# Down projection in seven products: second group's operands requested step by step, last operands of the first group ahead of a residual quarter

## The chip, the cores and the metric

The kernel runs on one core of a Trainium2 chip. The metric is the device time of one execution in microseconds. The times of the kernel before are those of three runs; the profile is that of one execution.

## What is computed

One step of a two-layer streaming encoder for 1024 prompt tokens and 32 sample tokens (1056 in all) of 1024 features, in float32. Layer 0 mixes with a matrix memory, layer 1 with banded attention; each is followed by the same kind of MLP, and the part of the reference that matters here is the MLP of layer 1 with its residual and norm:

```
x = layer_norm(ALPHA * x + (1 + g1) * y, p['ln_g'][l, 0], p['ln_b'][l, 0])
u = x * (1 + sc2) + sh2
f = jnp.square(jax.nn.relu(u @ p['w_up'][l])) @ p['w_down'][l]
x = layer_norm(ALPHA * x + (1 + g2) * f, p['ln_g'][l, 1], p['ln_b'][l, 1])
```

`w_up` is 1024 x 4096, `w_down` 4096 x 1024.

## The kernel before

Every float32 product is made of three matmuls on rounded halves: the high half of the weight with the high and the low half of the moving operand, then the low half of the weight with the high half. The halves are made by `split` (lines 87 to 90): a copy on ScalarE (L89) and a subtraction on VectorE (L90).

The MLP of layer 1 is `mlp7`. It cuts the 4096 hidden features into 16 blocks of 256 and the 1056 tokens into four quarters of 264, two quarters to a token pair. A 2 x 2 block product is made in seven products (`PRODS`, L1095) instead of eight. The up products write, for each hidden block, seven forms of the squared ReLU to DRAM (`hd`, L1172 and L1177), as high and low halves. The down products of blocks 0 to 13 follow in five groups (`GRP`, L1092): group 0 has two blocks, groups 1 to 4 have three each. Blocks 14 and 15 are done in the plain way at the end.

A **unit** (`unit`, L1394) is one group and one quarter `m` of the output features; there are four units to a group, numbered 0 to 3 for group 0, 4 to 7 for group 1 and so on. A unit has seven steps, and in each step a product for each of the two token pairs: six matmuls a product in group 0, nine in the others. In the very first unit the pair tp1 is not started until all seven products of tp0, the first pair in order, are done; everywhere else the pairs alternate. Behind each product VectorE adds the bank, times a gate, into the residual (`add_gated_at`, L986; the tile `ACX`), and a later step accumulates into the same bank, so it waits for that add.

Three kinds of transfers feed a unit, all of them from SP's queue, in the queue's order:

- the **operands** `fx`: fourteen sets for a group, one for each pair and form, loaded from `hd` by `Rooms.load` (L1107 to 1119). A set of group 0 is 128 x 1056 numbers, one of the others 128 x 1584. They are put into rooms: 56 slots in all, of which group 0 uses 28 and each other group 42. Nine sets of group 1 fit beside group 0; the other five take the rooms that unit 3 gives back, product by product (`after`, L1465). `fill` (L1383) asks for as many sets as there are rooms, or for as many as its last argument allows. A set whose slots lie in two tiles takes two transfers.
- the **weights** `rdn_d`: two transfers to a unit (L1248), into a ring of three buffers. `forms` (L1243 to 1275) makes the seven weight forms of them: differences on VectorE (L1264 to 1267), then splits. The tile names carry the unit's number: `rdn_d_3_0` is the first half for unit 3, `wf_d_3_4` the split forms 4 and 5 for it. A buffer comes free when VectorE has read it; the first half's last reader is L1266, the second half's the split of form 6.
- the **residual**, in four quarters (`reload`, L1932): the first two during the up products, the third (`L.reload(2)`) at the end of the up products, in `up_end` (L1420), the fourth (`L.reload(3)`) at the start of the down products (L1456). Units 0 and 1 add into the first half, unit 2 into the third quarter, unit 3 into the fourth.

TensorE's order is the order of the code (`manual_schedule`). The order of SP, VectorE and ScalarE is chosen by a scheduler when the kernel is built, from the order of the code and a model of the durations; on the chip each engine then works strictly in that order.

Of the kernel before, what the change touches and what calls it, by code (L numbers as in the profile page):

```python
# [75 lines left out]
def trunk_kernel(ctx: ExitStack, tc: tile.TileContext, a, o):  # L76
# [668 lines left out]
    for h in range(1, NH):  # L745
        unit = [0]
# [377 lines left out]
    def mlp7(L):  # L1124
# [204 lines left out]
        preps, got = {}, {}  # L1329

        def prep(n):
            if n < len(makers):
                preps[n] = makers[n]()
                next(preps[n])

        def advance(n, i):

            if n + 1 in preps and i in (0, 1, 3, 5):
                got[n + 1] = next(preps[n + 1])
            if i == 2:  # L1340
                prep(n + 2)
# [37 lines left out]
        fx, nfx, f4s = {}, {}, []  # L1379
# [3 lines left out]
        def fill(g, into, most=99):  # L1383

            kg = GRP[g][1]
            while want and len(rooms.free) >= kg and most:
                most -= 1
                if g >= len(GRP) - 3:
                    late = g == len(GRP) - 1 or g == len(GRP) - 2 and len(into) < 10
                    rooms.free.sort(key=lambda r: any(r[0] is t for t in f4s[:3]) == late)  # L1390
                tp, f = want.pop(0)
                into[tp, f] = rooms.load(hd[g][tp][f], kg)

        def unit(g, m, phases, ws, step, after):  # L1394


            kg = GRP[g][1]
            for tps in phases:
                ps = {}
                for i, (w, f, b, c, q) in enumerate(PRODS):  # L1400
                    for tp in tps:
                        first = (tp, b) not in ps
                        if first:
                            ps[tp, b] = mm(f"dn{l}_{g}_{m}_{tp}_{b}")
                        p = ps[tp, b][:, :QN]
                        for k in range(kg):
                            t, s0 = fx[tp, f][k]
                            for n_, (wl, xl) in enumerate(((0, 0), (0, 1), (1, 0))):
                                nc.tensor.matmul(p, ws[w][:, wl, k], t[:, s0, xl], start=first and k + n_ == 0,  # L1409
                                                 stop=k == kg - 1 and n_ == 2, skip_group_check=not first)  # L1410
                        L.add((2 * tp + q) * QN, QN, p, L.gate, 2 * m + c)
                        after(tp, f)
                        flow.tick(QN * kg / 768)
                    if tps is phases[-1]:
                        step(i)
# [2 lines left out]
        prep(1)  # L1418
        got[0] = next(preps[0])
        def up_end():  # L1420
            L.reload(2)
            for t in L.rooms(tp1):
                rooms.add(t)
            fill(0, fx)
        lone = max(j for j, (_, tp) in enumerate(jobs) if tp == tp0)
        sevens = {}
        with tc.manual_schedule(engines={mybir.EngineType.PE}):
# [16 lines left out]
        nu = len(seq)  # L1444
# [7 lines left out]
        with tc.manual_schedule(engines={mybir.EngineType.PE}):  # L1452
            for i, (g, m, phases) in enumerate(units):
                more = g + 1 < len(GRP)
                if i == 0:
                    L.reload(3)  # L1456
                if i == 0:
                    rooms.add(ring.tile([P, KG, 2, QN], F32R, tag="wc", name=f"fx_w{l}", bufs=6))
                    fill(0, fx)
                if m == 1 and more:  # L1460
                    want += [(tp, f) for f in order_f for tp in L.pairs]
                if m == (2 if g else 1) and more:
                    fill(g + 1, nfx)

                def after(tp, f):  # L1465
                    if m == 3 and more:
                        rooms.free += fx[tp, f]
                        fill(g + 1, nfx)
                unit(g, m, phases, got[nu + i], lambda j: advance(nu + i, j), after)
                if m == 3:  # L1470
                    assert not want
                    fx, nfx = nfx, {}
# [70 lines left out]
    for gi, grp in enumerate(((0, 1, 2), (3,))):  # L1543
        ws = {pr: [wblock(f"q{pr}_{half}", wq, 512 * half, 256 * pr) for half in range(2)] for pr in grp}
        for ti, (t0, n) in enumerate(TBS):
# [7 lines left out]
            for fc in [f for pr in grp for f in (2 * pr, 2 * pr + 1)]:  # L1553
                g, r = fc // 2, 2 * (fc % 2)
# [73 lines left out]
    for t in range(NT):  # L1628
        if t % 2 == 0 and t < 8:
            flow.add(cached_keys(t // 2))  # L1630
        m = P if t < NT - 1 else TS
# [279 lines left out]
    class L1:  # L1911
# [49 lines left out]
        def after(blk):  # L1961
            t0, n = blk
            tiles = [(t, min(P, t0 + n - t)) for t in range(t0, t0 + n, P)]
            flow.add(norm_out(tiles, L1.put_out, L1.next_y, L1.gb, blk == L1.blocks[-1]), TAIL[0])
    mlp7(L1)
    flow.finish()
    psD_cm.__exit__(None, None, None)
# [36 lines left out]
```

## Time and profile before

| what | us |
|---|---|
| median of 3 runs (lowest, highest) | 2462.29 (2459.95, 2464.19) |
| the profiled execution, its time | 2464.7 |
| its span, first to last instruction | 2462.6 |
| TensorE busy (share of the span) | 2387.9 (97%) |
| VectorE busy | 1918.8 (78%) |
| ScalarE busy | 1089.9 (44%) |
| first product of group 0 to the end of the down groups | 2077.5 to 2393 |
| mean granted TensorE clock | 0.989 |

The time of an execution is a little longer than its span, which counts from the first to the last instruction. In the rows of the profile an operation is named by its line, engine and tiles (written tile, arrow, read tiles); in the view in order of time a bracket at the end of a row gives the idle time of the engine just before it and what ended that time. A matmul's row carries the length of a run of matmuls, and `x` their number; matmuls overlap at their ends, so that the pace is read from one start to the next. `SPq` is SP issuing transfers: the row shows when one is issued, not when it lands.

### The profile page before, as it was taken

What the parts mean: (1) busy time and instruction counts of PE and PEld (TensorE: products, weight loads), DVE (VectorE), ACT (ScalarE), POOL (GpSimd) and SP (SyncE); (2) the same over time, 40 slices, a digit from 0 to 9 for tenths busy, and PEclk for the clock granted to TensorE, in tenths of its full rate; (3) what the DMA queues carried; (4) which work ended last, traced back from release to release, by engine and by line L of the source; (5) the groups of instructions that cost most, each with busy time, mean ns of one, the idle gap of its engine ahead of it and who ended that gap; (6) DMA issues with size and microseconds to landing.
All of it is one profiled execution on the core that took longest, in us unless ns stands there. A gap on an engine that the chain in (4) does not pass through costs nothing.

```text
span 2462.6 us, 42910 instructions
## 1 busy us (share of the span) xinstructions
PE 2387.9 (97%) x16580; PEld 2296.7 (93%) x16580; DVE 1918.8 (78%) x4340; ACT 1089.9 (44%) x2264; POOL 167.3 (7%) x315
## 2 busy tenths in 40 slices
PE   7999999999999999999999999999999999799997
PEld 4999999999999999999999977889999998799997
DVE  4899999788679679677497666755998888677778
ACT  4644456382212212212257566763776776122212
POOL 0211100000000000000001134410000000000003
PEclk9999999999999999999999999999999999899999
DMA  8433223313224224234123220051586789856642
GB/s 296 125 110 102 77 92 111 131 35 105 83 88 128 88 92 129 86 95 149 45 78 99 74 63 1 18 134 41 175 282 216 253 300 332 305 216 229 228 160 72
DMA packets 251504, 335.17 MB, mean 136 GB/s; under 512 B 12824, under 2 KB 201644, under 8 KB 250276
## 3 DMA queue, kind: packets, MB, share of 16 engines
q1 hardware_dynamic: 251300, 332.42, 41.2%
q8 instruction: 131, 2.15, 0.4%
q14 instruction: 73, 0.60, 0.1%
HBM read 255.50 MB, written 79.24 MB: 136 GB/s over the span
## 4 chain that ended last, share of the span: by engine, by line
PE 76%; DVE 11%; DMA 4%; ACT 2%; issue 2%; POOL 1%; SPq 0%; DVEq 0%; ACTq 0%; POOLq 0%
PE dn L1409 11%; PE up L1300 9%; PE up L118 5%; PE dn L119 5%; PE dn L118 5%; PE up L120 5%; PE up L119 5%; PE dn L120 5%; PE pv L1744 3%; PE s L1687 2%; PE pt L1722 2%; PE o L118 1%; PE o L119 1%; PE o L120 1%; PE op_b L118 1%
## 5 line engine op out<-in xcount | busy, mean ns | idle before, releaser
L1409 PE MATMUL dn<-fx,wf_d 128*128 128x264 f32 x2016 | 257.7, 288 | 17.2 <-DVE ACX L986 12.8
L1409 PEld LDWEIGHTS dn<-fx,wf_d 128*128 128x128 f32 x2016 | 252.8, 191 | 19.0 <-ACT wf_d L89 13.3
L119 PE MATMUL dn<-h,w_dn 128*128 128x384 f32 (+1 forms) x768 | 249.5, 325 | 0.0
L118 PE MATMUL up<-U,w_up 128*128 128x384 f32 (+1 forms) x768 | 249.2, 324 | 0.0
L119 PE MATMUL up<-U,w_up 128*128 128x384 f32 (+1 forms) x768 | 247.9, 323 | 0.0
L118 PE MATMUL dn<-h,w_dn 128*128 128x384 f32 (+1 forms) x768 | 247.8, 323 | 0.0
L120 PE MATMUL up<-U,w_up 128*128 128x384 f32 (+1 forms) x768 | 247.6, 322 | 0.0
L120 PE MATMUL dn<-h,w_dn 128*128 128x384 f32 (+1 forms) x768 | 247.3, 322 | 0.0
L986 DVE SCALAR_TENSOR_TENSOR ACX<-dn,ada,ACX 128x264 f32<-128x264 f32 (+5 forms) x400 | 160.7, 427 | 56.2 <-PE dn L1409 43.4
L238 DVE SCALAR_TENSOR_TENSOR aacc<-rada,cs,aacc 128x256 f32<-128x256 f32 x448 | 190.3, 478 | 0.0
L986 DVE SCALAR_TENSOR_TENSOR acc<-dn,ada,acc 128x384 f32<-128x384 f32 (+2 forms) x256 | 119.4, 486 | 47.6 <-PE dn L120 46.1
L1025 ACT ACTIVATE r<-up 128x384 f32<-128x384 f32 (+1 forms) x96 | 44.2, 462 | 243.5 <-PE up L120 238.2
L119 PEld LDWEIGHTS dn<-h,w_dn 128*128 128x128 f32 x768 | 144.5, 188 | 0.2 <-DVE h L1028 0.2
L120 PEld LDWEIGHTS dn<-h,w_dn 128*128 128x128 f32 x768 | 144.5, 188 | 0.0
L120 PEld LDWEIGHTS up<-U,w_up 128*128 128x128 f32 x768 | 144.3, 188 | 0.0
L118 PEld LDWEIGHTS up<-U,w_up 128*128 128x128 f32 x768 | 144.2, 188 | 0.1
L119 PEld LDWEIGHTS up<-U,w_up 128*128 128x128 f32 x768 | 144.2, 188 | 0.0
L118 PEld LDWEIGHTS dn<-h,w_dn 128*128 128x128 f32 x768 | 144.0, 187 | 0.2
L1300 PE MATMUL up<-u,wf_u 128*128 128x264 f32 x1056 | 139.5, 284 | 1.3 <-ACT wf_u L89 0.6
L1300 PEld LDWEIGHTS up<-u,wf_u 128*128 128x128 f32 x1056 | 132.6, 188 | 1.9 <-ACT wf_u L89 0.8
L1027 DVE TENSOR_TENSOR r<-r 128x384 f32<-128x384 f32 (+1 forms) x96 | 50.0, 523 | 102.3 <-ACT h L1026 101.9
L89 ACT CAST w_up<-raw_up 128x1024 fp32r<-128x1024 f32 x52 | 54.3, 1046 | 138.4 <-DMA raw_up<-in_w_up_dram 113.9
(386 smaller groups left out, 6569.4 us busy)
## 6 DMA issues: line engine op xcount, KB each, us to landing
rada<-in_w_ada_dram SPq DMA_DIRECT2D x64, 512.0 KB
hd<-HL SPq DMA_DIRECT2D x28, 1056.0 KB
raw_up<-in_w_up_dram SPq DMA_DIRECT2D x52, 512.0 KB
fx<-hd SPq DMA_DIRECT2D x50, 528.0 KB
hd<-HM SPq DMA_DIRECT2D x28, 792.0 KB
raw_dn<-in_w_down_dram SPq DMA_DIRECT2D x36, 512.0 KB
ada_room<-in_w_ada_dram SPq DMA_DIRECT2D x32, 512.0 KB
rdn_u<-in_w_up_dram SPq DMA_DIRECT2D x32, 512.0 KB
```

The costliest lines, as they stand in the source:

```text
L89: nc.scalar.copy(dst_h, src)
L118: nc.tensor.matmul(ps, wh, mov(0, k), start=(k == 0), stop=False)
L119: nc.tensor.matmul(ps, wh, mov(1, k), start=False, stop=False)
L120: nc.tensor.matmul(ps, wl, mov(0, k), start=False, stop=(k == nk - 1))
L238: nc.vector.scalar_tensor_tensor(acc[:, cnd], raw[:, k], sc, acc[:, cnd], op0=ALU.mult, op1=ALU.add)
L986: nc.vector.scalar_tensor_tensor(xs, ps[:, off + o:off + o + mm_], gate[:, fc, cnd:cnd + 1], xs, op0=ALU.mult, op1=ALU.add)
L1027: nc.vector.tensor_mul(r, r, r)
L1300: nc.tensor.matmul(p, self.ws[w][:, wl, k], moving(f, tp, xl, k), start=first and k + n_ == 0, stop=k == 3 and n_ == 2, skip_group_check=n ...
L1409: nc.tensor.matmul(p, ws[w][:, wl, k], t[:, s0, xl], start=first and k + n_ == 0, stop=k == kg - 1 and n_ == 2, skip_group_check=not first)
L1687: nc.tensor.matmul(s[:, b, :w], qst, kk[i][:, g, k0 + j0:k0 + j0 + w], start=(i == 0), stop=(i == 1))
L1722: nc.tensor.transpose(pt[:kp, j - j0, pr * P:(pr + 1) * P], ps_[pr][:, j * P:j * P + kp], ident)
L1744: nc.tensor.matmul(pv[64 * e:64 * e + 64, :nq], V[:kp, vt0 + j, g * 64:(g + 1) * 64], pts[e][:kp, j, :nq], start=(j == 0), stop=(j == nt - 1))
```

## The change

In `up_end` the third quarter of the residual is asked for after the rooms of the second token tile have been filled, no longer before. In the loop over the units, the `fill` for the second group (`g == 0`), which stood once at the start of unit 1 without a limit, is now made in units 1 and 2, behind each step, for one set at a time. For the later groups nothing is changed.

```
         def up_end():
-            L.reload(2)
             for t in L.rooms(tp1):
                 rooms.add(t)
             fill(0, fx)
+            L.reload(2)
...
-                if m == (2 if g else 1) and more:
+                if g and m == 2 and more:
                     fill(g + 1, nfx)
...
+                def step(j):
+                    advance(nu + i, j)
+                    if g == 0 and m in (1, 2):
+                        fill(g + 1, nfx, 1)
-                unit(g, m, phases, got[nu + i], lambda j: advance(nu + i, j), after)
+                unit(g, m, phases, got[nu + i], step, after)
```

The orders of TensorE and POOL stay as they were. The lines of code behind the change move down by five (L1937 becomes L1942). Three places show what the scheduler makes of it.

The first is SP's queue at the change from up to down products. `fx` are the operands (`hd_0` those of group 0, `hd_1` of group 1), `ACX<-xsp` the residual's quarters, `HL` and `HM` the forms of hidden block 13 going out. Before:

```order
L1937 DMA ACX_22648<-xsp_79 128x2112
L1117 DMA fx_22650<-hd_0_0_18338 128x1056 x4
L1172 DMA hd_4_0_18346<-HL_13_0_22656 128x4x528
L1177 DMA hd_4_0_18346<-HM_13_0_22663 128x3x528
L1937 DMA ACX_22648<-xsp_79 128x2112
L1248 DMA rdn_d_2_0_22777<-in_w_down_dram 128x2x256
L1248 DMA rdn_d_2_1_22779<-in_w_down_dram 128x2x256
L1117 DMA fx_22650<-hd_1_1_18341 128x1584
L1117 DMA fx_22650<-hd_1_0_18340 128x528
L1117 DMA fx_22650<-hd_1_0_18340 128x1056
L1117 DMA fx_22650<-hd_1_1_18341 128x1056
L1117 DMA fx_1_22672<-hd_1_1_18341 128x528
```

and with the change:

```order
L1117 DMA fx_22648<-hd_0_0_18338 128x1056 x4
L1942 DMA ACX_22653<-xsp_79 128x2112
L1172 DMA hd_4_0_18346<-HL_13_0_22656 128x4x528
L1177 DMA hd_4_0_18346<-HM_13_0_22663 128x3x528
L1942 DMA ACX_22653<-xsp_79 128x2112
L1248 DMA rdn_d_2_0_22777<-in_w_down_dram 128x2x256
L1248 DMA rdn_d_2_1_22779<-in_w_down_dram 128x2x256
L1117 DMA fx_22648<-hd_1_1_18341 128x1584
L1117 DMA fx_22648<-hd_1_0_18340 128x528
L1117 DMA fx_22648<-hd_1_0_18340 128x1056
L1248 DMA rdn_d_3_0_22886<-in_w_down_dram 128x2x256
L1248 DMA rdn_d_3_1_22888<-in_w_down_dram 128x2x256
```

The four operand loads have moved ahead of the third quarter, and the weights of unit 3 stand behind two operand sets of group 1 (three transfers). In the order before, those weights stood behind all nine sets but for a last piece. Before, a few rows further down:

```order
L1117 DMA fx_w_22679<-hd_1_1_18341 128x1584
L1248 DMA rdn_d_3_0_22896<-in_w_down_dram 128x2x256
L1248 DMA rdn_d_3_1_22898<-in_w_down_dram 128x2x256
L1248 DMA rdn_d_4_0_23034<-in_w_down_dram 128x3x256
L1117 DMA fx_w_22679<-hd_1_0_18340 128x528
L1248 DMA rdn_d_4_1_23036<-in_w_down_dram 128x3x256
```

With the change, at the same place:

```order
L1117 DMA fx_w_22679<-hd_1_1_18341 128x1584
L1248 DMA rdn_d_4_0_23034<-in_w_down_dram 128x3x256
L1248 DMA rdn_d_4_1_23036<-in_w_down_dram 128x3x256
L1117 DMA fx_w_22679<-hd_1_0_18340 128x528
L1117 DMA fx_e_21889<-hd_1_0_18340 128x1056
```

Behind the weights of unit 3 the other seven sets follow one another with nothing between, and behind them come both halves of the weights of unit 4, group 1's first.

The second place is VectorE in unit 2. `dn_0_2_1_0` is the bank of group 0, quarter 2, token pair 1, bank 0; the rows of L986 are the adds, the others make the weights of unit 3. Before:

```order
L986 TENSOR_SCALAR ACX_22648<-dn_0_2_0_1_22998,ada,ACX_22648 128x264
L90 TENSOR_TENSOR wf_d_3_0_22985<-rdn_d_3_0_22896,wf_d_3_0_22985 128x256
L1264 TENSOR_TENSOR s_d_3_23006<-rdn_d_3_0_22896,rdn_d_3_1_22898 128x256
L90 TENSOR_TENSOR wf_d_3_0_22985<-rdn_d_3_1_22898,wf_d_3_0_22985 128x256
L1265 TENSOR_TENSOR s_d_3_23007<-s_d_3_23006,rdn_d_3_0_22896 128x256
L1266 TENSOR_TENSOR s_d_3_23008<-rdn_d_3_0_22896 128x256
L1267 TENSOR_TENSOR s_d_3_23009<-rdn_d_3_1_22898,s_d_3_23007 128x256
L90 TENSOR_TENSOR wf_d_3_2_23014<-s_d_3_23007,wf_d_3_2_23014 128x256
L90 TENSOR_TENSOR wf_d_3_2_23014<-s_d_3_23006,wf_d_3_2_23014 128x256
L986 TENSOR_SCALAR ACX_22648<-dn_0_2_1_0_22969,ada,ACX_22648 128x232
L986 TENSOR_SCALAR ACX_22648<-dn_0_2_1_0_22969,ada,ACX_22648 128x32
L986 TENSOR_SCALAR ACX_22648<-dn_0_2_0_0_22977,ada,ACX_22648 128x264
```

and with the change:

```order
L986 TENSOR_SCALAR ACX_22653<-dn_0_2_0_1_22997,ada,ACX_22653 128x264
L986 TENSOR_SCALAR ACX_22653<-dn_0_2_1_0_22967,ada,ACX_22653 128x232
L986 TENSOR_SCALAR ACX_22653<-dn_0_2_1_0_22967,ada,ACX_22653 128x32
L986 TENSOR_SCALAR ACX_22653<-dn_0_2_0_0_22975,ada,ACX_22653 128x264
L90 TENSOR_TENSOR wf_d_3_0_22983<-rdn_d_3_0_22886,wf_d_3_0_22983 128x256
L1264 TENSOR_TENSOR s_d_3_23005<-rdn_d_3_0_22886,rdn_d_3_1_22888 128x256
L90 TENSOR_TENSOR wf_d_3_0_22983<-rdn_d_3_1_22888,wf_d_3_0_22983 128x256
L1265 TENSOR_TENSOR s_d_3_23006<-s_d_3_23005,rdn_d_3_0_22886 128x256
L1266 TENSOR_TENSOR s_d_3_23007<-rdn_d_3_0_22886 128x256
L1267 TENSOR_TENSOR s_d_3_23008<-rdn_d_3_1_22888,s_d_3_23006 128x256
L90 TENSOR_TENSOR wf_d_3_2_23013<-s_d_3_23006,wf_d_3_2_23013 128x256
L90 TENSOR_TENSOR wf_d_3_2_23013<-s_d_3_23005,wf_d_3_2_23013 128x256
```

The adds of the third step have moved ahead of the eight weight operations.

The third place is VectorE at the end of unit 3, where the weights of unit 4 are made. Before, their first splits stood among unit 3's first adds:

```order
L986 TENSOR_SCALAR ACX_22648<-dn_0_3_1_0_23107,ada,ACX_22648 128x264
L986 TENSOR_SCALAR ACX_22648<-dn_0_3_0_0_23117,ada,ACX_22648 128x264
L90 TENSOR_TENSOR wf_d_4_0_23125<-rdn_d_4_0_23034,wf_d_4_0_23125 128x384
L90 TENSOR_TENSOR wf_d_4_0_23125<-rdn_d_4_1_23036,wf_d_4_0_23125 128x384
L986 TENSOR_SCALAR ACX_22648<-dn_0_3_1_1_23130,ada,ACX_22648 128x264
```

With the change they stand behind unit 3's last adds:

```order
L986 TENSOR_SCALAR ACX_22653<-dn_0_3_0_0_23117,ada,ACX_22653 128x264
L90 TENSOR_TENSOR wf_d_4_0_23125<-rdn_d_4_0_23034,wf_d_4_0_23125 128x384
L1264 TENSOR_TENSOR s_d_4_23150<-rdn_d_4_0_23034,rdn_d_4_1_23036 128x384
L90 TENSOR_TENSOR wf_d_4_0_23125<-rdn_d_4_1_23036,wf_d_4_0_23125 128x384
L1265 TENSOR_TENSOR s_d_4_23151<-s_d_4_23150,rdn_d_4_0_23034 128x384
L1266 TENSOR_TENSOR s_d_4_23152<-rdn_d_4_0_23034 128x384
```

All eleven weight operations of unit 4 follow in one piece there, and the third pair of unit 3's own splits has moved behind the adds of unit 3's fourth step.

## The prediction

> **What bounds the kernel now.** The page comes first: the share of TensorE, then its costliest group.
>
> ```profile
> PE 2387.9 (97%) x16580; PEld 2296.7 (93%) x16580; DVE 1918.8 (78%) x4340; ACT 1089.9 (44%) x2264; POOL 167.3 (7%) x315
> L1409 PE MATMUL dn<-fx,wf_d 128*128 128x264 f32 x2016 | 257.7, 288 | 17.2 <-DVE ACX L986 12.8
> ```
>
> TensorE (PE) is the bound, so a time saved has to be idle or slow TensorE time. The second row, the down products, has 17.2 us of idle before it. Second view: TensorE's waits, first from 2075 to 2150 us (three rows), then from 2146 us to the end (the last).
>
> ```profile
> PE dn L1409 <- DVE ACX L986: 12.8, 3, 11.3
> PE dn L1409 <- DMA fx<-hd: 4.2, 2, 3.4
> PE dn L1409 <- DVE wf_d L90: 1.7, 1, 1.7
> PE dn L1409 <- DVE ACX L986: 1.2, 1, 1.2
> ```
>
> All but 1.2 us of it falls in the first group of down products; the other four run almost without a gap. Third view: TensorE in order of time (start, length, idle before).
>
> ```profile
> 2077.51 0.53 PE L1409 MATMUL dn<-fx_e,wf_d 128*128 128x264 f32 x3
> 2091.00 3.07 PE L1409 MATMUL dn<-fx,wf_d 128*128 128x264 f32 x12 [3.40 <-DMA fx<-hd]
> 2094.84 3.02 PE L1409 MATMUL dn<-fx,wf_d 128*128 128x264 f32 x12 [0.77 <-DMA fx<-hd]
> 2097.67 1.18 PE L1409 MATMUL dn<-fx_e,wf_d 128*128 128x264 f32 x6
> 2108.22 0.41 PE L1409 MATMUL dn<-fx_e,wf_d 128*128 128x264 f32 x2
> 2110.34 0.76 PE L1409 MATMUL dn<-fx_e,wf_d 128*128 128x264 f32 x4 [1.72 <-DVE wf_d L90]
> 2127.51 6.83 PE L1409 MATMUL dn<-fx,wf_d 128*128 128x264 f32 x36 [11.29 <-DVE ACX L986]
> 2134.18 0.89 PE L1409 MATMUL dn<-fx_e,wf_d 128*128 128x264 f32 x6
> 2141.55 13.41 PE L1409 MATMUL dn<-fx,wf_d 128*128 128x264 f32 x108 [1.37 <-DVE ACX L986]
> 2154.79 1.62 PE L1409 MATMUL dn<-fx_w,wf_d 128*128 128x264 f32 x12
> 2156.25 0.89 PE L1409 MATMUL dn<-fx_e,wf_d 128*128 128x264 f32 x6
> ```
>
> Twelve matmuls take 2156.25 - 2154.79 = 1.46 us, 0.122 each. A unit of group 0 has 84, so 10.25 us; a product has 6, 0.73 us. Units 1, 2 and 3 start at 2097.67, 2108.22 and 2134.18; unit 3's last 36 matmuls end at 2141.55 + 4.39 = 2145.94, where group 1 begins. After both long waits the matmuls are slow: 12 in 3.07 us, 36 in 2134.18 - 2127.51 = 6.67 us instead of 4.39. The granted clock (third from the end in each of these windows; behind it the DMA share and GB/s) says why:
>
> ```profile
> 2076.00:2084.00 8.00, 7.75 (x62) 7.35 (x60) 7.32 (x19) 5.89 (x11) 0.00 (x0) 1.00 0.97 324
> 2084.00:2092.00 8.00, 4.57 (x33) 4.10 (x31) 7.38 (x20) 3.16 (x6) 0.00 (x0) 0.97 1.03 374
> 2092.00:2096.00 4.00, 3.14 (x13) 2.58 (x13) 2.21 (x4) 0.50 (x2) 0.00 (x0) 0.50 1.00 345
> 2104.00:2122.00 18.00, 10.50 (x84) 10.08 (x83) 8.93 (x24) 2.45 (x7) 0.00 (x0) 0.91 1.03 404
> 2108.00:2112.00 4.00, 2.29 (x19) 2.07 (x18) 4.00 (x13) 1.63 (x5) 0.00 (x0) 1.00 1.04 420
> 2127.00:2134.00 7.00, 6.49 (x35) 6.52 (x36) 5.07 (x16) 0.41 (x1) 0.00 (x0) 0.61 0.16 55
> ```
>
> It fell to half after a gap of 3.40 us, but stayed full through the gap of 1.72 us. And the DMA engines are full all the way: what lands late was queued late. Fourth view: SP's queue, then ScalarE (ACT) and VectorE (DVE).
>
> ```profile
> 2080.34 2.54 SPq L1167 DMA_DIRECT2D hpl<-HL  x4
> 2082.97 0.56 SPq L1937 DMA_DIRECT2D ACX<-xsp  x1
> 2083.65 2.44 SPq L1117 DMA_DIRECT2D fx<-hd  x4
> 2094.70 2.30 SPq L1248 DMA_DIRECT2D rdn_d<-in_w_down_dram  x2
> 2097.04 13.54 SPq L1117 DMA_DIRECT2D fx<-hd  x12
> 2112.92 2.97 SPq L1248 DMA_DIRECT2D rdn_d<-in_w_down_dram  x3
> 2104.32 0.41 ACT L89 CAST wf_d<-rdn_d 128x256 fp32r<-128x256 f32 x1 [11.56 <-DMA rdn_d<-in_w_down_dram]
> 2123.62 0.41 ACT L89 CAST wf_d<-rdn_d 128x256 fp32r<-128x256 f32 x1 [12.60 <-DMA rdn_d<-in_w_down_dram]
> 2108.12 0.42 DVE L1264 TENSOR_TENSOR s_d<-rdn_d,rdn_d 128x256 f32<-128x256 f32 x1
> 2108.46 0.49 DVE L986 SCALAR_TENSOR_TENSOR ACX<-dn,ada,ACX 128x264 f32<-128x264 f32 x1
> 2112.22 1.68 DVE L986 SCALAR_TENSOR_TENSOR ACX<-dn,ada,ACX 128x264 f32<-128x264 f32 x4
> 2124.06 0.43 DVE L90 TENSOR_TENSOR wf_d<-rdn_d,wf_d 128x256 fp32r<-128x256 f32 x1 [10.16 <-ACT wf_d L89]
> 2126.75 1.94 DVE L986 SCALAR_TENSOR_TENSOR ACX<-dn,ada,ACX 128x232 f32<-128x232 f32 x6
> 2137.98 0.55 DVE L1264 TENSOR_TENSOR s_d<-rdn_d,rdn_d 128x384 f32<-128x384 f32 x1
> ```
>
> Read together: unit 3's weights (rdn_d_3) are asked for at 2112.92, behind twelve operand loads, and land at 2123.62. VectorE has their split in its order ahead of unit 2's third pair of adds, and stands before it for 10.16 us; TensorE's fifth pair of products accumulates into the bank that those adds read, and stands for 11.29 us. The cause is the place of a load in SP's queue.
>
> **The change, part by part.** TensorE's and POOL's orders don't change, nor the number of loads or bytes; what moves is SP's order and, with it, VectorE's and a little of ScalarE's.
>
> First, the residual's third quarter goes behind group 0's last four operand loads. They are issued at 2082.97 instead of 2083.65, 0.68 us earlier, and 128 x 2112 x 4 bytes = 1.08 MB no longer lie ahead: at the 374 GB/s of that window 2.9 us. So the eleventh operand lands at 2091.00 - 3.6 = 2087.4, where TensorE arrives at 2091.00 - 3.40 = 2087.60. The next follow at (2094.84 - 2091.00)/2 = 1.92 us; the fourteenth at 2087.4 + 5.8 = 2093.2, and unit 0 ends at about 2093.9 instead of 2097.67: **3.8 us** gained, with three waits of about 1.2 us in place of one long one. The quarter itself is read by unit 2's adds, 20 us later; that is its cover.
>
> Unit 1 then ends at 2104.2. Unit 2's weights have the same bytes ahead in the queue as before and land at 2104.32; cast 0.41 and subtraction 0.42 let TensorE start at about 2105.0. Before, it effectively started at 2110.34 - 0.24 = 2110.1. Gain so far **5.1 us**. From here VectorE does all eleven weight operations of unit 2 (2108.12 to 2112.22 with one add: 4.1 us) ahead of its first adds, so these come at 2109.2 where the third product wants its bank at 2108.1: a new wait of 1.1 to 1.2 us.
>
> Second, rdn_d_3 moves ahead of seven of the nine operand sets. Its second half takes the buffer that L1266 of unit 2 frees, and SP stands before it until about 2106.6. By then only two sets and the first half (1.9 MB, 4.6 us at 404 GB/s) lie behind 2104.32, so it lands at about 2110.2 and not 2123.62. VectorE, whose new order puts one more pair of adds ahead of it, gets there at 2111.4: **the 11.29 us wait goes, and with it the slow clock's 6.67 - 4.39 = 2.3 us**. What is late next: eight weight operations (2124.06 to 2126.75, 2.7 us) ahead of the fourth pair of adds cost the sixth pair of products about 1.2 us. Unit 2 takes 10.25 + 2.4, and unit 3 starts at 2117.7 instead of 2134.18: 16.5 us.
>
> Third, what is moved past. The seven sets (seven times 128 x 1584 x 4 bytes, 5.68 MB) now stand behind rdn_d_3 and ahead of rdn_d_4 (0.79 MB), which group 1's first unit needs: 6.47 MB at 404 GB/s are 16.0 us from 2110.2, so 2126.2. Unit 3 ends at 2117.7 + 10.25 + 1.0 = 2128.9; the 1.0 is the split of its third pair of weights, which VectorE now does only after the fourth pair of adds, and the 1.37 us wait of before goes. So the weights are there with 2.7 us to spare. Behind them SP has the five operand sets whose rooms unit 3 frees, used ten products later. The last of them, like the second half of rdn_d_5, now stands behind unit 4's L1266, near 2132; it is used at unit 4's fourteenth product, about 2144, so 12 us cover it. Gain 2145.94 - 2128.9 = 17.0 us.
>
> [...]
>
> Fourth, group 1's weights now come in one block after unit 3's last adds. TensorE waits an add and a subtraction (0.49 + 0.55), about 1.0 us, and at the third product about 0.9 us, since eleven operations of some 0.47 us net (5.2) stand ahead of the adds and two pairs of products last 4.4. Gain 17.0 - 1.9 = **15.1 us**. Behind this the work is TensorE's alone, by the 1.2 us of waits above, and everything moves up.
>
> The five small new waits (1.2, 1.2, 1.0, 1.0, 0.9: 5.3 us) are my working, shown by no row. Below, they could be nothing, but TensorE can't start group 1 before 2126.2 + 1.0, which caps the gain at 18.7 us; above, five of the largest of that kind seen (1.72) make 8.6 and a gain of 11.8. I keep 5.3, being nearest to the 1.2 and 1.37 us rows.
>
> [...]
>
> **The rivals.** (a) Group 1's weights come late. If the queue moves at the 324 GB/s of 2076 to 2084, 6.47 MB take 20.0 us: 2130.2, 0.7 us late; if SP also stands two or three microseconds longer before rdn_d_3's second half, group 1 starts 3 to 6 us later, and a gap of 3.40 us adds the slow clock's 2.3. Gain 6 to 12, so 2450 to 2456. For it: SP really stops there, with ten loads behind it. Against: 2.7 us of slack.
>
> (b) The trickle of unit 0 (TensorE at work 0.73 of every 1.92 us) lowers the clock. Unit 1 then loses about 2.3 to 2.5 us, with 0.1 us of slack at rdn_d_2: gain 12.6, 2449.7. Against: full clock through 1.72 us of idle.
>
> (c) Only the first part works; VectorE still stands before rdn_d_3. Gain 3.9, 2458.4. It needs rdn_d_3 to land later than it did; the new order speaks against it.
>
> (d) Slower: SP held at rdn_d_3's second half. Everything for group 1 is queued behind a buffer that VectorE frees, and group 1 starts some 20.5 us after the release (2110.2 - 2106.6, then 16.0, then 1.0). It decides from a release at 2145.94 - 20.5 = 2125.4; at 2132 the kernel is 6.6 us slower, 2469. That needs unit 2's weights over 20 us late, with the same bytes ahead of them: unlikely.
>
> **How the numbers follow.** The profiled execution has a span of 2462.6 us and a time of 2464.7; minus 15.1, 2447.5 and 2449.6. The median of the three runs, 2462.29, is 2.4 below that execution, so I forecast 2462.29 - 15.1 = 2447 us. Chances: forecast 0.62, (a) 0.18, (b) 0.07, (c) 0.07, (d) 0.06. The range takes in the forecast with its bounds (gain 11.8 to 18.7), (a) and (b): 2443 to 2457. About 0.2% is what a measurement can tell from no change, 4.9 us here; faster is the forecast with (a) and (b), 0.87; same is (c), 0.07; slower 0.06.
>
> **What would show it.** Right: no wait of TensorE over 2 us between 2080 us and group 1, no window at 0.50, VectorE's 10.16 us wait gone, rdn_d_3's cast near 2110, group 1 starting at about 2130. Wrong: a wait on wf_d_4 of several microseconds, SP standing before L1248 beyond 2108, or the lost time coming back in a later group as waits on operands.

## The result and the profile after

The changed kernel takes 2448.01 us (median of six runs, 2444.83 to 2451.64); the kernel before took 2463.61 in the six runs beside them. The ratio is 0.9936 [0.9921, 0.9951]: faster by 0.64%, 15.6 us, where 2447 us and a gain of 15.1 were forecast.

On the page of the profiled execution (span 2449.7 us, time 2451.64) TensorE is as busy as before, and the idle time before the down products has shrunk from 17.2 to 6.9 us:

```profile
PE 2386.9 (97%) x16580; PEld 2294.7 (94%) x16580; DVE 1919.8 (78%) x4340; ACT 1090.7 (45%) x2264; POOL 167.3 (7%) x315
L1409 PE MATMUL dn<-fx,wf_d 128*128 128x264 f32 x2016 | 254.2, 285 | 6.9 <-DVE ACX L986 3.3
```

TensorE's waits from 2075 to 2140 us (total, times, longest) show no wait over 1.2 us where one of 11.3 and one of 3.4 had been:

```profile
PE dn L1409 <- DVE ACX L986: 3.3, 4, 1.1
PE dn L1409 <- DVE wf_d L90: 2.0, 3, 0.8
PE dn L1409 <- DMA fx<-hd: 0.8, 2, 0.5
PE dn L1409 <- issue: 0.7, 1, 0.7
PE dn L1409 <- ACT wf_d L89: 0.4, 1, 0.4
```

TensorE in order of time (start, length, idle before):

```profile
2080.10 0.53 PE L1409 MATMUL dn<-fx_e,wf_d 128*128 128x264 f32 x3
2090.83 1.00 PE L1409 MATMUL dn<-fx,wf_d 128*128 128x264 f32 x6 [0.50 <-DMA fx<-hd]
2092.97 1.00 PE L1409 MATMUL dn<-fx,wf_d 128*128 128x264 f32 x6 [1.14 <-DVE ACX L986]
2096.54 0.89 PE L1409 MATMUL dn<-fx_e,wf_d 128*128 128x264 f32 x6
2107.38 1.22 PE L1409 MATMUL dn<-fx_e,wf_d 128*128 128x264 f32 x6 [0.44 <-ACT wf_d L89]
2109.90 0.89 PE L1409 MATMUL dn<-fx,wf_d 128*128 128x264 f32 x6
2111.70 4.62 PE L1409 MATMUL dn<-fx,wf_d 128*128 128x264 f32 x36 [0.91 <-DVE ACX L986]
2117.28 3.17 PE L1409 MATMUL dn<-fx,wf_d 128*128 128x264 f32 x24 [0.96 <-DVE ACX L986]
2120.29 0.89 PE L1409 MATMUL dn<-fx_e,wf_d 128*128 128x264 f32 x6
2122.48 4.05 PE L1409 MATMUL dn<-fx,wf_d 128*128 128x264 f32 x32
2127.21 4.66 PE L1409 MATMUL dn<-fx,wf_d 128*128 128x264 f32 x36 [0.67 <-DVE wf_d L90]
2132.67 4.43 PE L1409 MATMUL dn<-fx,wf_d 128*128 128x264 f32 x34 [0.81 <-DVE wf_d L90]
2137.80 4.63 PE L1409 MATMUL dn<-fx,wf_d 128*128 128x264 f32 x36 [0.70 <-issue]
2157.65 1.70 PE L1409 MATMUL dn<-fx_w,wf_d 128*128 128x264 f32 x12
```

Units 1, 2 and 3 start at 2096.54, 2107.38 and 2120.29, and group 1, behind its first wait, at 2132.67. These times can't be set beside those of before as they stand: the two executions were already 2.59 us apart at the first down product (2080.10 against 2077.51), behind code that the change leaves alone. That is why the spans differ by only 12.9 us. So every time below is given **from the first down product of its own execution**, with a plus: unit 1 +16.44 (before +20.16), unit 3 +40.19 (+56.67), and the end of the span +369.60 (+385.09), a gain of 15.5 us. By the start of the wide operands (`fx_w`) in unit 5, at +77.55, 15.1 of it is there (before, 2170.12, +92.61): nothing is given back later.

The transfers and those who wait for them: SP's queue, ScalarE's first copies for units 2, 3 and 4, and VectorE where it reaches the weights of units 3 and 4.

```profile
2085.72 2.13 SPq L1117 DMA_DIRECT2D fx<-hd  x4
2087.90 0.47 SPq L1942 DMA_DIRECT2D ACX<-xsp  x1
2101.78 7.82 SPq L1248 DMA_DIRECT2D rdn_d<-in_w_down_dram  x2
2106.92 0.40 ACT L89 CAST wf_d<-rdn_d 128x256 fp32r<-128x256 f32 x1 [12.03 <-DMA rdn_d<-in_w_down_dram]
2112.98 0.41 ACT L89 CAST wf_d<-rdn_d 128x256 fp32r<-128x256 f32 x1 [0.23 <-DMA rdn_d<-in_w_down_dram]
2128.12 0.51 ACT L89 CAST wf_d<-rdn_d 128x384 fp32r<-128x384 f32 x1 [8.64 <-DMA rdn_d<-in_w_down_dram]
2129.17 0.51 ACT L89 CAST wf_d<-rdn_d 128x384 fp32r<-128x384 f32 x1 [0.53 <-DMA rdn_d<-in_w_down_dram]
2113.84 0.41 DVE L90 TENSOR_TENSOR wf_d<-rdn_d,wf_d 128x256 fp32r<-128x256 f32 x1
2132.07 0.55 DVE L90 TENSOR_TENSOR wf_d<-rdn_d,wf_d 128x384 fp32r<-128x384 f32 x1
```

Unit 3's weights are all there at 2112.98, +32.9 (before, the first half came at +46.1), and VectorE comes to them at 2113.84 without a bracket: it no longer waits. The row of L1248 shows SP standing 7.82 us over the two halves, as foreseen, until their buffer is free; 5.6 us of it is SP's wait for VectorE's L1266. Unit 4's second half is copied at 2129.17, 2.9 us before VectorE comes to that unit's weights. From the first down product to unit 5 the granted clock was full (1.00) in every half microsecond, and until about +62 the DMA engines were full but for single half microseconds (the lowest share 0.54). Two stretches show it (third from the end the clock, then DMA share and GB/s):

```profile
2092.00:2096.00 4.00, 2.23 (x14) 1.87 (x15) 4.00 (x10) 1.13 (x2) 0.00 (x0) 1.00 1.05 409
2110.00:2122.00 12.00, 10.13 (x82) 9.76 (x81) 10.90 (x32) 3.02 (x8) 0.00 (x0) 1.00 1.01 385
```

### The profile page after: what moved, and what is told of

Same layout as the page of the kernel before. It is cut to its first block, busy times and chain, and to the rows that moved or that the text cites. A ratio compares the mean times of both kernels' runs of the same rounds, so it can differ in the third digit from the quotient of the medians.

```text
span 2449.7 us, 42910 instructions
## 1 busy us (share of the span) xinstructions
PE 2386.9 (97%) x16580; PEld 2294.7 (94%) x16580; DVE 1919.8 (78%) x4340; ACT 1090.7 (45%) x2264; POOL 167.3 (7%) x315
## 4 chain that ended last, share of the span: by engine, by line
PE 76%; DVE 12%; DMA 4%; ACT 3%; issue 2%; POOL 0%; SPq 0%; ACTq 0%; DVEq 0%; POOLq 0%
PE dn L1409 11%; PE up L1300 6%; PE up L118 6%; PE up L120 6%; PE up L119 6%; PE dn L119 5%; PE dn L118 5%; PE dn L120 5%; PE pv L1749 3%; PE s L1692 2%; PE pt L1727 2%; PE o L118 1%; PE o L119 1%; PE o L120 1%; DMA hd<-HL 1%
## 5 line engine op out<-in xcount | busy, mean ns | idle before, releaser
L986 DVE SCALAR_TENSOR_TENSOR ACX<-dn,ada,ACX 128x264 f32<-128x264 f32 (+5 forms) x400 | 160.1, 426 | 52.6 <-PE dn L1409 39.6
L986 DVE SCALAR_TENSOR_TENSOR acc<-dn,ada,acc 128x384 f32<-128x384 f32 (+2 forms) x256 | 119.2, 485 | 47.0 <-PE dn L120 45.6
```

Of the source, the lines that this page charges most:

```text
L986: nc.vector.scalar_tensor_tensor(xs, ps[:, off + o:off + o + mm_], gate[:, fc, cnd:cnd + 1], xs, op0=ALU.mult, op1=ALU.add)
```

## The experiments

The theory: what decides is the **place of each unit's weights in SP's queue**, with the DMA engines full ahead of it, and where VectorE, strictly in order, first needs them; every such stop holds the adds queued behind it (before, VectorE stood 10.16 us ahead of unit 3's split and TensorE 11.29 us for the adds behind it). The rivals: the first part (the residual's third quarter) does the work; one set per step, the thin stream, is what helps; VectorE's load is the bound. "To the end" is the time from the first down product to the end of the span in the one profiled execution.

| run | ratio to before | to the end, us | longest wait in units 2 to 4, us |
|---|---|---|---|
| before | 1 | 385.1 | 11.29 |
| the change | 0.9936 [0.9921, 0.9951] | 369.6 | 0.96 |
| the change again | 0.9939 [0.9927, 0.9951] | 370.3 | 0.96 |
| e1, quarter only | 0.9997 [0.9988, 1.0007] | 383.9 | 12.15 |
| e2, steps only | 0.9946 [0.9931, 0.9961] | 373.2 | 1.30 |
| e3, nine behind the weights | 0.9977 [0.9966, 0.9987] | 378.2 | 8.48 |
| e4, five first | 0.9967 [0.9955, 0.9980] | 378.2 | 7.01 |
| e5, fourth quarter later | 0.9946 [0.9934, 0.9958] | 369.0 | 2.12 |
| e6, e3 with e5 | 0.9973 [0.9964, 0.9982] | 378.5 | 9.32 |
| e7, unit 3's forms on GpSimd | 1.0001 [0.9992, 1.0010] | 382.3 | 6.11 |
| e8, bursts behind weights | 0.9952 [0.9939, 0.9966] | 371.8 | 1.61 |
| e9, later start and quarter | 0.9947 [0.9932, 0.9961] | 372.5 | 1.25 |

Each ratio is to runs of the kernel before made beside that run. From the wide operands in unit 5 to the end, all twelve profiled executions take 291.5 to 292.7 us; a larger difference between runs comes from ahead of this mark.

**The change again.** 

> The change itself once more, on the same chip as the two kernels that go beyond it. Group 1 starts 52.3 us after the first down product, with the same five small waits; ratio to before 0.992 to 0.995.

It came out the same: 2449.26 us, the five waits 0.91, 0.96, 0.68, 0.81 and 0.73 us long, and group 1 at +53.0, 0.7 us later than expected. The two executions of one kernel differ by 0.7 us to the end, so that a difference of this size is scatter.

**e1: the first part alone.**

```
         def up_end():
-            L.reload(2)
...
             fill(0, fx)
+            L.reload(2)
```

> Only the first part: the residual's third quarter behind the first group's last operands; the nine operand sets of the second group at once, as before. SP's order then has the weights of unit 3 behind all nine sets, as before. My theory (the weights of unit 3 land behind full DMA engines, and VectorE stands before them with the adds behind it): unit 0 gains its 3.8 us, but the weights of unit 3 have the same bytes ahead of them and land as late as before, about 46 us after the first down product; TensorE reaches the blocked bank earlier and waits there about 14 to 15 us instead of 11.3. Group 1 starts 67 to 69 us after the first down product (68.4 before, 52.3 with the change); time 0 to 1 us below before, ratio 0.9995 to 1.0005. Rival, as my prediction priced it (the first part keeps its gain by itself): group 1 starts at 64.6 us, 3.8 us below before.

No difference in time. Unit 0 ends 3.4 us sooner (unit 1 at +16.80), but the wait in unit 2 grows from 11.29 to 12.15 us, as TensorE's row in order of time shows, and unit 2 starts with a wait of 2.14 us; unit 3's weights land at +45.3, hardly sooner than before (+46.1):

```profile
2103.43 0.76 PE L1409 MATMUL dn<-fx_e,wf_d 128*128 128x264 f32 x4 [2.14 <-DVE wf_d L90]
2122.97 6.92 PE L1409 MATMUL dn<-fx,wf_d 128*128 128x264 f32 x36 [12.15 <-DVE ACX L986]
```

The wait is shorter than the 14 to 15 us that I expected, because part of the time won goes ahead of it: unit 2 starts with the 2.14 us, and behind them the matmuls are slow: six take 1.16 us and the next six 1.33 (starts at 2104.02, 2105.18 and 2106.51), where 0.73 is full pace. Unit 3 starts at +55.9 (before +56.67), sooner by no more than the weights land sooner. Time won ahead of a late transfer is waited away in front of it.

**e2: the second part alone.**

```
-                if m == (2 if g else 1) and more:
+                if g and m == 2 and more:
                     fill(g + 1, nfx)
...
+                    if g == 0 and m in (1, 2):
+                        fill(g + 1, nfx, 1)
```

> Only the second part: one set per step in units 1 and 2; the residual's third quarter stays ahead of the first group's last operands. My theory: the wait of 3.4 us for the operands in unit 0 and the half clock behind it stay, so that unit 1 ends about 30.4 us after the first down product and hides the landing of unit 2's weights (26.8); the wait behind VectorE goes. Group 1 starts at 54 to 56 us (68.4 before, 52.3 with the change), so 12 to 14 us below before, ratio about 0.9945. Rival (the two parts add up, 3.8 from the first): 56.1 us or more. Rival (the second part works only because the first made room on the DMA engines): the weights of unit 3 come late and TensorE waits 5 us or more in unit 2.

As expected: 11.9 us of the 15.5, and group 1 at +55.5. Unit 2 has no wait over 1.30 us; that of unit 0 stays (TensorE in order of time):

```profile
2089.79 3.06 PE L1409 MATMUL dn<-fx,wf_d 128*128 128x264 f32 x12 [3.94 <-DMA fx<-hd]
```

So the first part is worth nothing alone and, in the traces, some 3 us behind the second (373.2 against 369.6 and 370.3; the intervals of the ratios overlap): the gains don't add, they follow one another along the queue.

**e3: all nine sets in one go, but behind unit 3's weights** (the rest as in the change).

```
-                    if g == 0 and m in (1, 2):
-                        fill(g + 1, nfx, 1)
+                    if g == 0 and m == 1 and j == 2:
+                        fill(g + 1, nfx)
```

> Both parts, but the nine sets are again asked for at once, in unit 1 behind the step that asks for unit 3's weights. SP's order: first half of those weights, one set, second half, then the other eight sets together. My theory (only the place of unit 3's weights in the queue counts, not that the sets come singly): group 1 starts 51 to 53 us after the first down product, within 1.5 us of the change, no wait of TensorE over 2 us; ratio to before about 0.9935. Rival (asking step by step itself, a thinner stream, is what helps): the weights of unit 3 or of group 1's first unit are late again, with a wait of 5 us or more, and group 1 starts beyond 57 us.

A miss. Unit 2 runs through, but the same stop returns one unit later. TensorE, ScalarE and VectorE in order of time:

```profile
2125.53 18.55 PE L1409 MATMUL dn<-fx,wf_d 128*128 128x264 f32 x132 [8.48 <-DVE ACX L986]
2123.87 0.51 ACT L89 CAST wf_d<-rdn_d 128x384 fp32r<-128x384 f32 x1 [11.65 <-DMA rdn_d<-in_w_down_dram]
2124.42 0.56 DVE L90 TENSOR_TENSOR wf_d<-rdn_d,wf_d 128x384 fp32r<-128x384 f32 x1 [9.67 <-ACT wf_d L89]
```

Unit 4's weights, now behind the nine sets, land at +50.8. VectorE stands before their split from +41.7, because in this kernel, as in the one before, that split stands among unit 3's first adds. I had looked only at unit 3's weights. In the change they land only 2.8 us sooner (+48.0), but it has moved VectorE's operations on them behind unit 3's adds, where VectorE comes at +52.0: that is why it can keep seven sets ahead of them. e8 tests the other way out, an earlier landing.

**e4: five sets first, then one per step.**

```
+                if g == 0 and m == 1:
+                    fill(g + 1, nfx, 5)
```

> Both parts, but five sets are asked for at the start of unit 1 and the rest one per step. SP's order has seven sets ahead of unit 3's weights (two with the change, nine before). VectorE's order has the first operation on these weights behind the adds of unit 2's sixth step, and the last split of unit 2's own weights behind that. My theory: the weights land at about 42 us after the first down product (32.8 with the change, 46.1 before); VectorE holds no add but holds the last split of unit 2, so TensorE waits at unit 2's last step for about 6 to 7 us, partly followed by half clock; group 1 starts at 58 to 61 us, so 8 to 10 us below before, ratio about 0.9962. Rival (the wait of before was the bank waiting for adds alone, and goes as soon as VectorE has the adds ahead): no wait over 2 us inside unit 2, only one at the start of unit 3. Rival (landing counts little): within 2 us of the change.

As expected, in size and place: five more sets ahead of unit 3's weights delay them to +43.1, and unit 2's last step waits 7.01 us, with slow matmuls behind it (six in 1.32 us, from 2123.69 to 2125.01, where 0.73 is full pace). Group 1 starts at +61.9, just beyond the 58 to 61 expected. TensorE in order of time, then ScalarE's copy of those weights:

```profile
2121.33 2.57 PE L1409 MATMUL dn<-fx,wf_d 128*128 128x264 f32 x10 [7.01 <-DVE wf_d L90]
2118.65 0.40 ACT L89 CAST wf_d<-rdn_d 128x256 fp32r<-128x256 f32 x1 [11.78 <-DMA rdn_d<-in_w_down_dram]
```

One set per step does not help by itself: here the last four are asked for that way.

**e5: the change, and the residual's fourth quarter one unit later.**

```
-                if i == 0:
+                if i == 1:
                     L.reload(3)
```

> The change, and besides the residual's fourth quarter (1.08 MB) asked for at the start of unit 1 instead of unit 0, which puts it behind unit 2's weights in SP's queue. My theory (with full DMA engines a landing is the sum of the bytes ahead of it): unit 2's weights land 2.7 us earlier, about 24.1 us after the first down product instead of 26.8, the waits of 0.44 and 0.91 us at the start of unit 2 go, and group 1 starts 1 to 2 us earlier than with the change, at 50.3 to 51.3 us. In the time 1 to 2 us, which a comparison may not tell from the change. Rival (landing is set by when SP comes to issue, not by the bytes ahead): the weights land within 1 us of before.

Unit 2's weights land at +24.05 instead of +26.8, and the wait of 0.44 us goes; that of 0.91 does not, it becomes 1.19. Group 1 starts at +48.8, sooner than expected. But its first unit, unit 4, then waits 1.14 and 2.12 us, and over the change 0.6 us are left in the trace, no more than scatter, and nothing in time. The 2.12 us are not a late transfer: unit 5's weights land at +58.0, sooner than in the change (+58.8), and VectorE does not wait for them. VectorE's order has changed too: it begins the eleven operations on them at +61.1 (in the change +64.0), ahead of the adds that unit 4's last step needs. ScalarE's copies for units 2 and 5, then TensorE:

```profile
2099.74 0.41 ACT L89 CAST wf_d<-rdn_d 128x256 fp32r<-128x256 f32 x1 [9.39 <-DMA rdn_d<-in_w_down_dram]
2133.65 0.51 ACT L89 CAST wf_d<-rdn_d 128x384 fp32r<-128x384 f32 x1 [5.27 <-DMA rdn_d<-in_w_down_dram]
2141.76 11.21 PE L1409 MATMUL dn<-fx,wf_d 128*128 128x264 f32 x90 [2.12 <-DVE ACX L986]
```

**e6: nine behind the weights, with e5's later quarter.**

```
+                    if g == 0 and m == 1 and j == 2:
+                        fill(g + 1, nfx)
...
-                if i == 0:
+                if i == 1:
                     L.reload(3)
```

> The nine sets at once behind the request for unit 3's weights, and the fourth quarter at the start of unit 1. Unit 3's weights then stand in SP's queue ahead of all nine sets, behind only the fourth quarter. My theory: nothing of group 0 waits for a transfer any more but the last operands of unit 0; group 1 starts at 49.5 to 51.5 us after the first down product, unless group 1's first weights, now behind all nine sets (7.3 MB, 18 us from the release of unit 3's buffer), land after TensorE is there: they would land at about 47 us, 2 us ahead of it. Rival: these weights come late and give 1 to 4 us back.

A miss. The wait in unit 3 stays, 9.32 us. The profile names ScalarE's copy of unit 4's weights as what ended it, but the products of unit 3 don't use these. It is the stop of e3: VectorE stands before their split, with the next adds of unit 3 behind it:

```profile
2132.51 0.56 DVE L90 TENSOR_TENSOR wf_d<-rdn_d,wf_d 128x384 fp32r<-128x384 f32 x1 [10.52 <-ACT wf_d L89]
```

Unit 4's weights land at +50.9, as in e3, and not at about +47: one quarter of the residual (1.08 MB) does not make up for nine sets (7.3 MB). The rival had the direction right, but what is given back, to the end and against the change, is 8.9 us and not 1 to 4.

**e7: the kernel before, with unit 3's differences and subtractions on GpSimd.**

```
-        def forms(src, kg, nm):
+        def forms(src, kg, nm, eng=None):
+            ve = eng or nc.vector
...
-            nc.vector.tensor_add(s1, a21, a22)
+            ve.tensor_add(s1, a21, a22)
...
-                "(k s p) c -> s p k c", s=2, p=P)[s_], kg, f"d{l}_{i}")
+                "(k s p) c -> s p k c", s=2, p=P)[s_], kg, f"d{l}_{i}", nc.gpsimd if i == 3 else None)
```

> The kernel before, but the differences and subtractions that make unit 3's weights run on GpSimd instead of VectorE; SP's order as before, so that these weights land as late as before (46.1 us after the first down product). My theory: VectorE no longer holds the adds, so TensorE goes through unit 2 without the wait of 11.3 us and waits only at the start of unit 3, some 4 to 6 us, until the weights are there; GpSimd is slower (0.6 to 1.4 us for the sizes around it in the profile before), and VectorE's order has an operation on unit 4's weights early, which gives part of it back. Group 1 starts at 60 to 65 us, 4 to 8 us below before. Rival (TensorE waits for the weights as such, and VectorE's order is no matter): the wait is as long as before and group 1 starts at 68 us or later.

The weights land as late as before (+46.1), but with them on an engine that has no adds behind it the 11.29 us stop of unit 2 is gone, and unit 3 starts at +46.6 (before +56.67): that stop was VectorE's order, not the transfer itself. But the gain is 2.8 us to the end in the trace (1.8 at the wide operands of unit 5) and none in the time, and not 4 to 8: TensorE waits 4.40 us for the weights at unit 3's start, and 6.11 us later on, since VectorE now stands 13.99 us before unit 4's. TensorE, then VectorE in order of time (a line of code more than before):

```profile
2112.81 8.23 PE L1410 MATMUL dn<-fx,wf_d 128*128 128x264 f32 x66
2125.43 0.51 PE L1410 MATMUL dn<-fx_e,wf_d 128*128 128x264 f32 x2 [4.40 <-ACT wf_d L89]
2136.81 17.70 PE L1410 MATMUL dn<-fx,wf_d 128*128 128x264 f32 x132 [6.11 <-DVE ACX L986]
2132.63 0.96 DVE L1265 TENSOR_TENSOR s_d<-rdn_d,rdn_d 128x384 f32<-128x384 f32 x1 [13.99 <-DMA rdn_d<-in_w_down_dram]
```

**e8: the change in two bursts, each behind the next weights.**

```
-                    if g == 0 and m in (1, 2):
-                        fill(g + 1, nfx, 1)
+                    if g == 0 and m in (1, 2) and j == 2:
+                        fill(g + 1, nfx, 5 if m == 1 else 99)
```

> The nine sets go in two bursts, four or five at a time, each behind the request for the weights of the next unit, instead of one per step. Theory of place (what counts is how many bytes stand ahead of each unit's weights on SyncE's queue, and where VectorE first needs them): rdn_d_3 has one set ahead of it instead of two and lands by +33 after the first down product; rdn_d_4 has four sets and its own 0.79 MB behind rdn_d_3, 4.0 MB at 0.4 MB per us, so it lands at +41 to +43, while VectorE reaches its first operation on it at about +42 (in this order these operations stand among unit 3's adds again, as with nine behind the weights). So the waits of TensorE stay at 2 us or below each, and from the first down product to the end it takes 369 to 371 us, as with the change (369.6 and 370.3): no difference from it in time. Rival, the thin stream (one set per step is what keeps the transfers from standing in each other's way): a burst of four or five sets holds up a unit's weights, a wait of 5 us or more in unit 3, and the time is 5 to 9 us over the change's, as it was with nine behind the weights.

No wait over 1.61 us: the thin stream falls as the explanation of a gain of this size. The landings came about as expected (unit 4's weights at +42.4 and +43.5; ScalarE's row has the first half), and VectorE, whose operations on them stand among unit 3's adds as in e3, though a few adds later, comes at +44.5 (there +41.7) and does not wait:

```profile
2119.74 0.51 ACT L89 CAST wf_d<-rdn_d 128x384 fp32r<-128x384 f32 x1 [2.31 <-DMA rdn_d<-in_w_down_dram]
2121.77 0.55 DVE L1264 TENSOR_TENSOR s_d<-rdn_d,rdn_d 128x384 f32<-128x384 f32 x1
2130.07 10.46 PE L1409 MATMUL dn<-fx,wf_d 128*128 128x264 f32 x84 [1.61 <-DVE ACX L986]
```

With e3 this separates the two halves: early on VectorE and late on the queue costs 8.48 us; early on both, nothing of the kind. Had VectorE come as early as in e3, it would have stood an estimated 1.2 us (until the copy that starts at +42.4 has taken its 0.51). It ends at 371.8, 0.8 us above what I expected, with waits of 0.9 to 1.6 us on VectorE's adds and splits. The intervals of this ratio and the change's overlap, so that a small worth of the thin stream stays open.

**e9: the change begun at the third step, with e5's later quarter.**

```
-                if i == 0:
+                if i == 1:
                     L.reload(3)
...
-                    if g == 0 and m in (1, 2):
+                    if g == 0 and m in (1, 2) and j >= 2:
                         fill(g + 1, nfx, 1)
```

> The change, with its stream begun only at the third step of unit 1 and of unit 2, behind the weights of the next unit, and with the fourth quarter of the residual also asked for one unit later. Theory of place: rdn_d_2 lands at +24 as in the run with the later fourth quarter, rdn_d_3 with only that quarter ahead of it at +29 to +31, rdn_d_4 with five sets behind rdn_d_3 at +42 to +45. The waits at the start of units 2 and 4 of the change's trace (0.4 and 0.8 us) go, a wait of 1 to 2 us at unit 5 stays, as it was there with the later quarter, because rdn_d_5 stands where it stood: 368 to 370 us from the first down product to the end, 0 to 2 us below the change. Rival: VectorE, not the transfers, sets the pace once no weights are late; then nothing is won at all, and the waits on its adds grow by what the waits on weights lose.

A miss: 372.5. Unit 3's weights were all there at +33.3 and not at +29 to +31, unit 4's first half at +46.4. SP's queue in order of time says why, a window (at its end clock, DMA share and GB/s) what the DMA engines did meanwhile, and the third view has a wait of TensorE in unit 5:

```profile
2098.35 11.86 SPq L1248 DMA_DIRECT2D rdn_d<-in_w_down_dram  x2
2110.27 4.86 SPq L1117 DMA_DIRECT2D fx<-hd  x7
```

```profile
2100.00:2110.00 10.00, 10.00 (x84) 10.00 (x83) 8.11 (x22) 1.74 (x5) 0.00 (x0) 1.00 0.56 210
```

```profile
2154.10 4.62 PE L1409 MATMUL dn<-fx,wf_d 128*128 128x264 f32 x36 [1.16 <-DVE ACX L986]
```

SP stood before the second half of unit 3's weights until their buffer came free (VectorE's L1266 ended at 2109.78, SP's row at 2110.21), and this time no operand sets had been issued ahead of it: from 2100 to 2110 the DMA engines were busy for 0.56 of the time, where they were full in the change (1.01 from 2100.8 to 2110.8). But VectorE comes to these weights after they have landed, and no wait of TensorE on them grew. Unit 1 began 1.9 us later than in the change, by the clock (below); by the wide operands of unit 4 all but 0.35 us of that was won back. The time was lost behind them, 2.4 us by the wide operands of unit 5, in waits on adds of 1.16 and 0.85 us that the change does not have. The first stands behind unit 5's weights, which VectorE makes in one block that it begins only at +68.6 (in the change at +64.0), at the start of unit 5; the second behind unit 6's. VectorE does not wait for unit 5's weights there either. So this run bears out a part of the rival: with no weights late, VectorE's order sets what is left.

## Why the prediction was right

- **Unit 0's end** (forecast: 3.8 us). 20.16 became 16.44: 3.72. But not by three waits on operands of 1.2 us: in this execution the operands cost 0.50 and 0.30, VectorE's late add 1.14 and its late weights 0.49. That the sum comes so close is luck in part; the eleventh operand let TensorE go at +10.7, where +10.1 was forecast, and the same code gains 3.3 in its second profile.
- **Unit 2's start** (5.1 us). Its weights were there at +26.82, as before at +26.81. Its second product starts at 2108.44, +28.3 (before 2110.94, +33.4): 5.1 us were gained.
- **Unit 3's weights** (forecast at +32.7, VectorE there at +33.9, SP held until +29.1). Measured +32.9, +33.7, and SP's row ends at +29.5. Unit 3 began 16.5 us sooner, as forecast. This is the step on which the result rests. Where the weights stay late (e1 +45.3, e4 +43.1), TensorE stands 12.15 and 7.01 us in unit 2; where they are early (e2 +34.3, e3 +32.3), unit 2 has no wait over 1.30 us. Early weights with VectorE's old order in unit 2 were not run.
- **The five small waits** (1.1 to 1.2, 1.2, 1.0, 1.0, 0.9: 5.3 us). All five are there, in their places. Their brackets (0.91, 0.96, 0.67, 0.81, 0.70) add up to 4.05 us, but a bracket counts only the idle time. From one start to the next, less 0.122 us for each matmul, the five cost 1.07, 1.19, 0.83, 1.07 and 0.98: 5.14 us. For the first, 2111.70 - 2109.90 = 1.80 us for six matmuls that take 0.73. The profile gives no cause for the last ("issue"); VectorE's first add behind the eleven weight operations starts at 2137.22, just ahead of it.
- **Unit 4's weights** (+48.7, 2.7 us to spare). +48.0 and +49.1, 2.9 to spare. From 2112.98 to 2129.17, in 16.2 us, the queue moved 6.47 MB, 400 GB/s against the 404 that I used. Rival (a) needed 324 GB/s and a longer stop of SP, (d) a far longer one; neither came.
- **Group 1's start** (+51.4 and 1.0 more): +52.57. At the wide operands of unit 4 the gain is 15.1 us (+62.2 against +77.3).

Of the rivals, (c) was **priced wrong**: the first part alone gives no 3.9 us. e1 shows the late landing taking it back, since the fixed time was that of unit 3's weights and not the length of unit 2's wait. (b) did not come in this execution; in the second one of the same code the clock did fall at the end of unit 0, at a price of 0.4 us and not of 2.3 to 2.5, as the next section shows.

## What the runs showed of the hardware

The granted clock fell without an idle stretch as long as 3.40 us. In the second profile of the change, the same code as above, TensorE's waits at the end of unit 0 were 1.45 and 0.39 us, and then the clock was half. TensorE in order of time, then the windows:

```profile
2088.35 1.01 PE L1409 MATMUL dn<-fx,wf_d 128*128 128x264 f32 x6 [1.45 <-DMA fx<-hd]
2089.74 4.08 PE L1409 MATMUL dn<-fx,wf_d 128*128 128x264 f32 x18 [0.39 <-DMA fx<-hd]
2093.66 0.89 PE L1409 MATMUL dn<-fx_e,wf_d 128*128 128x264 f32 x6
```

```profile
2090.00:2093.00 3.00, 3.00 (x15) 2.84 (x15) 2.84 (x7) 0.85 (x1) 0.00 (x0) 0.50 1.00 348
2093.00:2097.00 4.00, 4.00 (x33) 4.00 (x33) 2.77 (x7) 0.00 (x0) 0.00 (x0) 0.95 1.03 399
```

The 18 matmuls took 3.92 us (2093.66 - 2089.74) where 2.19 is full pace, and unit 1 began at +16.85 instead of +16.44: only 0.4 us is lost, since the slow matmuls fill time that would have been waits. So the prediction's argument against rival (b), full clock through 1.72 us of idle, does not hold in general, and that no window at 0.50 came, its sign of being right, was chance in the first profile. The drop came in the executions of e1, e3, e4 and e8 too, after gaps of 1.3 to 1.6 us, and for twice as long in e9, after one of 1.46 us, where unit 1 began at +18.30; it did not come in the change's first profile, e5 and e6, although e6 had a gap of 1.77 us. Added up from the clock of windows of one microsecond, taken as half or full, these low stretches lasted 3.40 to 3.42 us, and 6.82 in e9; before the change, behind the gap of 3.40 us, it was 6.8. What sets these lengths, when a stretch begins, and how much work keeps the clock up, these runs don't settle.

## What to carry to other kernels

When an in-order engine makes operands out of late transfers and also frees another engine's buffers, read two orders together: how many bytes stand ahead of each load on its queue, and what stands behind the load's first reader. A change to the queue is worth what the next late load leaves of it: look one load further (e3, 8.48 us one unit later), and time won ahead of a fixed landing is no gain (e1, ratio 0.9997). Once no load is late, the place of the in-order engine's own work among the operations that free buffers sets what is left (a wait of 2.12 us in e5, of 1.16 and 0.85 in e9). Compare executions from a common mark behind the unchanged code, and not by span.
